# A Hawk and Conformer step: the order of every engine and the place of every tile taken from a list schedule in the source

## The chip, the cores and the metric

The kernel runs on one core of a Trainium2 chip. The core has five engines with their own instruction streams: TensorE (PE) for matrix products, VectorE (DVE), ScalarE (ACT), GpSimd (POOL), and SyncE (SP), which here only starts transfers. They meet at semaphores. The metric is the device time of one execution in microseconds; lower is better.

## The reference

1056 tokens (1024 of a prompt, then 8 samples of 4) go through two layers, each x + Mixer(RMSNorm(x)), and a last RMSNorm. D is 1024, the inner width 2048.

```python
# layer 0, Hawk
u = rmsnorm(x, g) @ w_in                      # [.., 4096]
xb, z = u[..., :2048], u[..., 2048:]
xb = causal_dwconv(xb, w of 4 taps) + b
r = sigmoid(einsum('bthi,hij->bthj', xb, w_a) + b_a)      # 16 blocks of 128 x 128
i = sigmoid(einsum('bthi,hij->bthj', xb, w_i) + b_i)
log_a = -8 * r * softplus(-lam);  a = exp(log_a)
b = sqrt(-expm1(2 * log_a)) * (i * xb)
h_t = a_t * h_(t-1) + b_t                     # scan over tokens
x = x + (h * silu(z)) @ w_out
# layer 1, Conformer
v, gl, z = split(rmsnorm(x, g) @ w_in + b_in)
c = v * sigmoid(gl)
c = silu(layernorm(causal_dwconv(c, w of 31 taps) + b))
x = x + (c * silu(z)) @ w_out + b_out
y = rmsnorm(x)
```

The states of both convolutions and of the scan are outputs too.

## The kernel before

Channels lie on the 128 partitions, tokens along the row. The 1056 tokens form three chunks of C = 352, one PSUM bank each. Inner channels form 16 blocks of 128, numbered s in layer 0 and j in layer 1. Weights come in slabs of 128 x 1024.

Products are made in a rounded 32-bit format with both sides split into a high part (a copy on ScalarE) and a low part (a subtraction on VectorE or GpSimd). So each term is three products, `high*high`, `high*low`, `low*high` (`mm`, three lines of matmuls). `w_conv` makes a slab's parts wh and wl. For 38 slabs of layer 1 the low part is made during layer 0 (`pre_low`: preh on ScalarE, pre on VectorE or GpSimd, then a store).

Layer 0, for each block s:

- X: three units of 24 products give xp, one for each chunk (`xb_unit`); ScalarE copies them to pad (`xb_evac`). `conv0` does the four taps (first on ScalarE into acc, then VectorE, the last into xc), `xc_split` the parts xcsh and xcsl.
- Z: three units give zp, `z_evac` puts SiLU of each chunk into zs.
- G: six gate units gp (`gate_unit`), three products and one sigmoid each, give r and i. `chain` goes on in steps q: 0 exponential a and tanh; 1 products on VectorE; 2 square root; 3 q times i; 4 the scan; 5 times zs; 6 the split into gsh and gsl. For block 15 steps 5 and 6 go by chunk.
- O: for a pair of blocks, half of its out products at a time: `out_unit`, six products into one bank op, and `out_evac`, in which VectorE adds the bank to x1.

The order by blocks is X4, Z4, O of an earlier pair, G4, and so on; the last steps are FINAL. The last two pairs' products go by chunk, together with the second norm (st: sums of squares by products; pb: the result spread over partitions). Layer 1 makes v, gl and z; cpad holds v times the sigmoid, spad the samples. VectorE does most of the 31 taps into cv, ScalarE and GpSimd 9 of them (prod, part). LayerNorm, the last products yp and the final norm follow.

Banks, tiles and order: 4 PSUM banks (mm) rotate among xp, zp, op and layer 1's products, 4 others (aux) among gates and sums. Rows of tokens live in 42 slots and 2 quick ones, small things in 10. A tile pool hands out places in rotation; who gets a used one waits for its last reader. Everything is put down as an event, and the sorted events are run:

```python
def at(t, fn, *a):
    ev.append((t, len(ev), fn, a))
for engines, a, b in ((SU_E, -1e9, SU_M), ((), SU_M, t_ordered), (MAN, t_ordered, 1e9)):
```

Before t = SU_M = 46 (startup) and from t_ordered on (the last chunks), the order of the events is each engine's order. Between them the framework's own scheduler reorders instructions by its estimate of when each could start. The three lines show the three stretches.

## Time and profile before

| | |
|---|---|
| Median of 3 runs | 1466.67 us (1466.05 to 1466.89) |
| Span of the profiled execution, first to last instruction | 1462.3 us |
| The runs' median less that span | 4.4 us |
| TensorE busy | 1398.0 us, 96% |
| VectorE busy | 1161.8 us, 79% |
| ScalarE, GpSimd busy | 872.4 and 872.5 us, 60% each |
| Mean granted TensorE clock | 0.986 |
| HBM read and written | 128.77 and 46.22 MB |

The profile is of one execution; the span leaves out what lies before the first and behind the last instruction. Busy time is the time in instructions, waiting is not counted. The granted clock is the share of full speed at which TensorE was let run. A line number is that of the kernel's source. A row of the timeline has start, duration, engine, line, operation, output and inputs; in brackets the idle time before it and what ended it. A row of a stretch gives for every engine its busy time with the number of instructions, then the clock, the DMA share and GB/s.

### The profile page before, as it was taken

What the parts mean: (1) busy time and instruction counts of PE and PEld (TensorE: products, weight loads), DVE (VectorE), ACT (ScalarE), POOL (GpSimd) and SP (SyncE); (2) the same over time, 40 slices, a digit from 0 to 9 for tenths busy, and PEclk for the clock granted to TensorE, in tenths of its full rate; (3) what the DMA queues carried; (4) which work ended last, traced back from release to release, by engine and by line L of the source; (5) the groups of instructions that cost most, each with busy time, mean ns of one, the idle gap of its engine ahead of it and who ended that gap; (6) DMA issues with size and microseconds to landing.
All of it is one profiled execution on the core that took longest, in us unless ns stands there. A gap on an engine that the chain in (4) does not pass through costs nothing.

```text
span 1462.3 us, 21525 instructions
## 1 busy us (share of the span) xinstructions
PE 1398.0 (96%) x8525; PEld 1367.2 (93%) x8525; DVE 1161.8 (79%) x1274; ACT 872.4 (60%) x1132; POOL 872.5 (60%) x479
## 2 busy tenths in 40 slices
...
GB/s 262 26 40 52 62 148 134 134 162 119 141 147 129 124 156 110 87 24 182 157 72 92 106 77 205 103 133 110 112 117 141 92 88 131 243 172 189 76 0 119
...
## 3 DMA queue, kind: packets, MB, share of 16 engines
...
q14 instruction: 34, 0.28, 0.1%
HBM read 128.77 MB, written 46.22 MB: 120 GB/s over the span
## 4 chain that ended last, share of the span: by engine, by line
DVE 25%; PE 22%; POOL 5%; issue 3%; ACT 3%; DMA 2%; SPq 0%; POOLq 0%; DVEq 0%; ACTq 0%
DVE cv__9086 L870 2%; DVE cv__10890 L870 2%; DVE cv__9391 L870 2%; DVE cv__8787 L870 2%; POOL part__7852 L832 1%; DMA co<-od 1%; DVE cv__10602 L870 1%; POOL part__8145 L832 1%; DVE co L1089 1%; DVE cv__7518 L870 1%; DVE cpad L816 1%; DVE cv__9687 L870 1%; DVE cv__11218 L870 1%; DVE cv__8491 L870 1%; DVE co L1085 1%
## 5 line engine op out<-in xcount | busy, mean ns | idle before, releaser
L827 ACT ACTIVATE prod<-cpad,lay 128x1024 f32<-128x1024 f32 x119 | 135.7, 1147 | 64.1 <-POOL part__8145 L832 7.7
L530 DVE SCALAR_TENSOR_TENSOR acc<-pad,par,acc 128x1080 f32<-128x1080 f32 x32 | 62.5, 1961 | 39.6 <-ACT acc L523 39.2
L612 POOL COPY st_h<-r 128x1 f32<-128x1 f32 x16 | 17.4, 1090 | 103.6 <-DVE r L611 103.6
L336 POOL TENSOR_TENSOR pre<-pre,preh 128x1024 f32<-128x1024 f32 x19 | 49.5, 2607 | 48.2 <-ACT preh L335 37.4
L542 POOL TENSOR_TENSOR gsl<-zs,gsh 128x1056 fp32r<-128x1056 f32 x15 | 37.1, 2474 | 26.3 <-ACT gsh L541 23.3
L1152 POOL TENSOR_TENSOR sq<-sq 128x512 f32<-128x512 f32 (+2 forms) x20 | 19.0, 953 | 56.4 <-ACT sq L1148 56.2
L1148 ACT ACTIVATE sq<-x 128x512 f32<-128x512 f32 (+2 forms) x23 | 11.4, 501 | 67.5 <-DVE x L1138 63.6
L336 DVE TENSOR_TENSOR pre<-pre,preh 128x1024 f32<-128x1024 f32 x19 | 30.3, 1593 | 26.2 <-ACT preh L335 26.2
L541 ACT ACTIVATE gsh<-zs 128x1056 fp32r<-128x1056 f32 x15 | 16.3, 1084 | 56.2 <-DVE zs L618 56.2
L541 ACT ACTIVATE xcsh<-xc 128x1056 fp32r<-128x1056 f32 x16 | 17.4, 1086 | 53.6 <-DVE xc L535 53.6
L894 POOL TENSOR_TENSOR sum<-sum,co 128x1056 f32<-128x1056 f32 x13 | 35.0, 2689 | 23.9 <-DVE co L870 15.4
L1093 ACT ACTIVATE co<-co,par 128x352 f32<-128x352 f32 (+1 forms) x24 | 22.7, 970 | 41.8 <-DVE co L1089 41.8
L335 ACT ACTIVATE preh<-pre 128x1024 fp32r<-128x1024 f32 x38 | 40.0, 1052 | 12.8 <-DMA pre<-win 12.6
L400 POOL TENSOR_TENSOR hl<-hn,hh 128x352 fp32r<-128x352 f32 x24 | 25.4, 1062 | 36.5 <-ACT hh L397 31.0
L879 POOL TENSOR_TENSOR smp<-spad,lay 128x992 f32<-128x992 f32 x16 | 40.1, 2504 | 4.3 <-DVE spad L815 4.3
L944 POOL TENSOR_TENSOR ssq<-ssq,sq 128x1056 f32<-128x1056 f32 x14 | 40.6, 2897 | 0.0
L594 DVE TENSOR_TENSOR i<-i,xc 128x1056 f32<-128x1056 f32 x16 | 31.4, 1965 | 10.2 <-ACT i L582 9.1
L604 DVE TENSOR_TENSOR q<-q,i 128x1056 f32<-128x1056 f32 x16 | 21.7, 1356 | 21.9 <-ACT q L601 21.9
L611 DVE TENSOR_TENSOR_SCAN r<-a,q 128x1056 f32<-128x1056 f32 x16 | 37.7, 2357 | 0.6
L1105 POOL TENSOR_TENSOR nl<-co,nh 128x1056 fp32r<-128x1056 f32 x6 | 16.6, 2767 | 34.3 <-ACT nh L1101 31.8
L1085 DVE TENSOR_TENSOR co<-co,mub 128x1056 f32<-128x1056 f32 (+1 forms) x20 | 25.3, 1289 | 10.8 <-DMA co<-od 7.9
L393 DVE SCALAR_TENSOR_TENSOR hn<-x,par,pb 128x352 f32<-128x352 f32 x48 | 25.5, 573 | 9.6 <-PE pb L285 5.2
...
## 6 DMA issues: line engine op xcount, KB each, us to landing
...
```

What stands on the lines that cost most here:

```text
L335: act.activation(h, r, AF.Copy)
L336: (dve if early[i] % PRED == PRED - 1 else pool).tensor_sub(r, r, h.bitcast(F))
L530: dve.scalar_tensor_tensor(acc, pad[:, k:k + n], w, acc, op0=OP.mult, op1=OP.add)
L541: act.activation(h, src, AF.Copy)
L542: lo.tensor_sub(l, src, h.bitcast(F))
L611: dve.tensor_tensor_scan(h, B["a", s], B["q", s], 0.0, op0=OP.mult, op1=OP.add)
L827: act.activation(p, B["c", j][:, k:k + NP], AF.Identity, scale=dw(j, k), bias=P("dw_b", j) if k == 0 else 0.0)
L870: dve.scalar_tensor_tensor(o, x, dw(j, k), y, op0=OP.mult, op1=OP.add)
L879: pool.tensor_mul(t_.rearrange("p (b t w) -> p b t w", b=NB, t=NS), win, wb)
L894: pool.tensor_add(B["sum"], B["sum"], B["o", j])
L944: (dve if j in SQD else pool).tensor_add(B["ssq"], B["ssq"], q)
L1085: dve.tensor_sub(d, d, B["mu", 0][:, :C] if c == 0 else B["mub"][:, w])
```

## The change

All engine calls are now recorded (`Eng`, `Plan.record`) instead of issued: each becomes an `Op` with an estimated duration, the operations it must follow (from the ranges of tiles that it reads and writes), and the tiles it needs. Consecutive matmuls of one event are one Op. `Plan.schedule` then builds the order of all five engines. The event time is an Op's due time, pulled ahead where a successor needs it earlier. At each step every engine looks at its next few Ops by due time (3 for PE, 30, 30, 20, 12), takes the first, or a later one that fits in before it; the earliest over all engines is placed. It accounts for table loads (1.3 us), for VectorE operations with two SBUF inputs and GpSimd's excluding each other, and for a DMA rate. A place (44 slots, 10 small ones, 4 + 4 banks) is given when an Op first needs it, the one that is free longest, and each has a tag of its own. `emit` issues everything in that order, for all five engines, from first to last.

```diff
+    def record(self, eng, name, fn, args, kw):
+        merge = eng == "PE" and self.last and self.last[0].eng == "PE" and self.last[1] == self.event
...
+        for o in ops:
+            o.due = o.at + SHIFT.get(o.key, 0.0)
+        for o in reversed(ops):
+            for s in o.succ:
+                o.due = min(o.due, s.due - o.dur - MARGIN - (T_DMA0 + T_DMAX + o.dma / DMA_BW if o.dma else 0))
...
+                    x = T_TABLE if o.func and o.func != table else 0.0
+                    s = max((max(free[e], last_end[e]) + x) if x else free[e], o.ready, c)
+                    if o.lock:
+                        s = max(s, lock)
+                    opts.append((s, x, o))
...
+                pick = opts[0]
+                for q in opts[1:]:
+                    back = T_TABLE if q[1] and pick[2].func and pick[2].func == table else 0.0
+                    if q[0] + q[2].dur + back + q[1] * 0.5 <= pick[0] + FIT[e]:
+                        pick = q
+                        break
+                s, x, o = pick
+                if best is None or s < best[0]:
+                    best = (s, x, o)
...
+    def emit(self, make, warm):
+        for o in self.seq:
+            for t in o.new:
+                t.real = make(t)
+            if o.warm:
+                warm(o.kind)
+            for fn, args, kw in o.parts:
+                fn(*[real(a) for a in args], **{k: real(a) for k, a in kw.items()})
...
+WIN = {"PE": 3, "DVE": 30, "Activation": 30, "Pool": 20, "SP": 12}
+LOOK = {"DVE": 20.0, "Activation": 20.0, "Pool": 20.0, "SP": 20.0}
+FIT = {"PE": 0.1, "DVE": 0.2, "Activation": 0.2, "Pool": 0.4, "SP": 0.1}
...
+        def warm(func):
+            nc.scalar.activation(spare.get()[:, 1:2], spare.get()[:, 0:1], func)
...
         def z_evac(s, c):
-            act.activation(B["zs", s][:, cs(c)], ps[:, :C], AF.Silu)
+            act.activation(B["zs", s][:, cs(c)], ps[:, :C], AF.Copy)
         def z_silu(s):
-            act.activation(B["zs", s][:, :C], B["zs", s][:, :C], AF.Silu)
+            act.activation(B["zs", s], B["zs", s], AF.Silu)
-        def gate_unit(s, u):
-            g, c = divmod(u, NCH)
...
-            ps = aux(f"gp{s}_{u}_")[:, :C]
-            mm(ps, [(h[:, g * 128:g * 128 + 128], l[:, g * 128:g * 128 + 128], xh[:, cs(c)], xl[:, cs(c)])])
...
+        def gate_units(s, g):
...
+            ps = [aux(f"gp{s}_{g}_{c}_")[:, :C] for c in range(NCH)]
+            for c in range(NCH):
+                mm(ps[c], [(h[:, g * 128:g * 128 + 128], l[:, g * 128:g * 128 + 128], xh[:, cs(c)], xl[:, cs(c)])])
+            for c in range(NCH):
+                act.activation(B["ri"[g], s][:, cs(c)], ps[c], AF.Sigmoid, bias=P("b_a" if g == 0 else "b_i", s))
...
             elif q == 2:
                 act.activation(B["q", s], B["q", s], AF.Sqrt)
+                if s not in late_z:
+                    z_silu(s)
...
-        flush(t_man)
+        flush()
```

`warm` puts a one-column activation on a constant tile `spare` ahead of each operation of another table, so that the table's load stands with it. SiLU of z is taken on the whole row of 1056 behind the square root of its block (behind its last z chunk in blocks 14 and 15). TensorE's 8472 matmuls are the same in number. Table loads are 91 instead of 101, with 90 one-column activations; 16 SiLUs of a whole row are added. On SP eight loads of x stand ahead of the first slab; before, it stood ahead of them; of neighbouring taps on VectorE, 101 pairs are on one accumulator instead of 64. Now every line of an engine's instruction is that of `emit` (L378) or `warm` (L455).

TensorE around the first gate of block 9, before (op3_4_1, for instance, is pair 3, out block 4, chunk 1; gp9_0 the first gate unit; the names behind are high and low parts):

```order
L244 MATMUL op3_4_2__3647<-gsh7_3139,wh27__3514 128x352
L245 MATMUL op3_4_2__3647<-gsl7_3140,wh27__3514 128x352
L246 MATMUL op3_4_2__3647<-gsh7_3139,wl27__3516 128x352
L244 MATMUL gp9_0__3731<-xcsh9_3582,gwh_3588 128x352
L245 MATMUL gp9_0__3731<-xcsl9_3583,gwh_3588 128x352
L246 MATMUL gp9_0__3731<-xcsh9_3582,gwl_3589 128x352
L244 MATMUL gp9_1__3739<-xcsh9_3582,gwh_3588 128x352
L245 MATMUL gp9_1__3739<-xcsl9_3583,gwh_3588 128x352
L244 MATMUL op3_5_0__3655<-gsh6_2769,wh27__3514 128x352
L245 MATMUL op3_5_0__3655<-gsl6_2770,wh27__3514 128x352
L246 MATMUL op3_5_0__3655<-gsh6_2769,wl27__3516 128x352
```

and after:

```order
L378 MATMUL op3_6_1_.0_3735<-gsh7.0_3290,wh27_.0_3453 128x352
L378 MATMUL op3_6_1_.0_3735<-gsl7.0_3294,wh27_.0_3453 128x352
L378 MATMUL op3_6_1_.0_3735<-gsh7.0_3290,wl27_.0_3486 128x352
L378 MATMUL gp9_0_0_.0_3743<-xcsh9.0_3670,gwh.9_3483 128x352
L378 MATMUL gp9_0_0_.0_3743<-xcsl9.0_3690,gwh.9_3483 128x352
L378 MATMUL gp9_0_0_.0_3743<-xcsh9.0_3670,gwl.9_3520 128x352
L378 MATMUL gp9_0_1_.0_3744<-xcsh9.0_3670,gwh.9_3483 128x352
L378 MATMUL gp9_0_1_.0_3744<-xcsl9.0_3690,gwh.9_3483 128x352
L378 MATMUL gp9_0_1_.0_3744<-xcsh9.0_3670,gwl.9_3520 128x352
L378 MATMUL gp9_0_2_.0_3745<-xcsh9.0_3670,gwh.9_3483 128x352
L378 MATMUL gp9_0_2_.0_3745<-xcsl9.0_3690,gwh.9_3483 128x352
L378 MATMUL gp9_0_2_.0_3745<-xcsh9.0_3670,gwl.9_3520 128x352
```

Before, three out products (op3_4_0 to op3_4_2) of that half stand between the last z product and the gate; after, eight (op3_4_0 to op3_6_1), and the gate's three chunks stand together, where op3_5_0 stood amid the second.

ScalarE at the end of layer 0, before (zp15_2 is the last z product, q15 the square root's row):

```order
L591 ACTIVATE a15_5791<-r15_5727,c8_79 128x1056
L592 ACTIVATE r15_5727<-r15_5727,c8_79 128x1056
L569 ACT_TABLE_LOAD
L569 ACTIVATE zs15_5798<-zp15_0__5760 128x352
L227 ACTIVATE wh46__5825<-wraw46__5765 128x1024
L569 ACTIVATE zs15_5798<-zp15_1__5800 128x352
L601 ACT_TABLE_LOAD
L601 ACTIVATE q15_5795<-q15_5795 128x1056
L569 ACT_TABLE_LOAD
L569 ACTIVATE zs15_5798<-zp15_2__5835 128x352
L227 ACTIVATE wh47__5865<-wraw47__5863 128x1024
L623 ACTIVATE gsh15_5870<-zs15_5798 128x352 x3
```

and after:

```order
L455 ACTIVATE spare_80<-spare_80 128x1
L378 ACTIVATE a15.0_5929<-r15.0_5838,c8_73 128x1056
L378 ACTIVATE r15.0_5838<-r15.0_5838,c8_73 128x1056
L378 ACTIVATE zs15.0_5857<-zp15_2_.0_5898 128x352
L378 ACTIVATE wh48_.0_5941<-wraw48_.0_5887 128x1024
L455 ACT_TABLE_LOAD
L455 ACTIVATE spare_80<-spare_80 128x1
L378 ACTIVATE q15.0_5944<-q15.0_5944 128x1056
L455 ACT_TABLE_LOAD
L455 ACTIVATE spare_80<-spare_80 128x1
L378 ACTIVATE zs15.0_5857<-zs15.0_5857 128x1056
L378 ACTIVATE gsh15.0_5962<-zs15.0_5857 128x352 x3
```

The square root stood ahead of the last z chunk's evacuation and a weight conversion, and stands behind both now; the whole row's SiLU and its table load stand between it and gsh15.

VectorE when the out products of pair 4 begin, before (x1_0 is out block 0; xcsl10 is the low part of block 10's convolution, pre a low part of layer 1's weights):

```order
L542 TENSOR_TENSOR xcsl10_3951<-xc10_3947,xcsh10_3950 128x1056
L646 TENSOR_TENSOR x1_0_88<-op4_0_0__3995,x1_0_88 128x352
L646 TENSOR_TENSOR x1_0_88<-op4_0_1__4003,x1_0_88 128x352
L646 TENSOR_TENSOR x1_0_88<-op4_0_2__4015,x1_0_88 128x352
L336 TENSOR_TENSOR pre_4046<-pre_4046,preh_4108 128x1024
L646 TENSOR_TENSOR x1_1_89<-op4_1_0__4023,x1_1_89 128x352
L646 TENSOR_TENSOR x1_1_89<-op4_1_1__4031,x1_1_89 128x352
L646 TENSOR_TENSOR x1_1_89<-op4_1_2__4039,x1_1_89 128x352
L646 TENSOR_TENSOR x1_2_90<-op4_2_0__4049,x1_2_90 128x352
L646 TENSOR_TENSOR x1_2_90<-op4_2_1__4057,x1_2_90 128x352
```

and after:

```order
L378 TENSOR_TENSOR x1_0.0_87<-op4_0_0_.0_4039,x1_0.0_87 128x352
L378 TENSOR_TENSOR x1_0.0_87<-op4_0_1_.0_4053,x1_0.0_87 128x352
L378 TENSOR_TENSOR x1_0.0_87<-op4_0_2_.0_4065,x1_0.0_87 128x352
L378 TENSOR_TENSOR xcsl10.0_4083<-xc10.0_4036,xcsh10.0_4063 128x1056
L378 TENSOR_TENSOR x1_1.0_89<-op4_1_0_.0_4075,x1_1.0_89 128x352
L378 TENSOR_TENSOR x1_1.0_89<-op4_1_1_.0_4087,x1_1.0_89 128x352
L378 TENSOR_TENSOR x1_1.0_89<-op4_1_2_.0_4095,x1_1.0_89 128x352
L378 TENSOR_TENSOR x1_2.0_92<-op4_2_0_.0_4103,x1_2.0_92 128x352
L378 TENSOR_TENSOR x1_2.0_92<-op4_2_1_.0_4111,x1_2.0_92 128x352
L378 TENSOR_TENSOR pre.23_4005<-pre.23_4005,preh.23_4073 128x1024
L378 TENSOR_TENSOR x1_2.0_92<-op4_2_2_.0_4133,x1_2.0_92 128x352
```

The first three additions to x1 stood behind xcsl10 and stand ahead of it now; a subtraction of pre stands between additions in both.

More of the change, by code (lines that the diff above doesn't have):

```diff
@@ L91, with __init__, _with, __getitem__ @@
 RMS_EPS, LN_EPS = 1e-6, 1e-5
+class V:
+    def __init__(self, tile_, ops, idx):
+        self.tile, self.ops, self.idx = tile_, ops, idx
+    def _with(self, op, idx):
+        return V(self.tile, self.ops + (op,), idx)
+    def __getitem__(self, key):
+        return self._with(lambda a: a[key], self.idx[key])
+    def bitcast(self, dt):
+        return self._with(lambda a: a.bitcast(dt), self.idx)
+    def to_broadcast(self, shape):
+        return self._with(lambda a: a.to_broadcast(shape), self.idx)
+    def rearrange(self, pat, **kw):
+        left = pat.split("->")[0]
+        shape = self.idx.shape
+        if "(" in left:
+            names = left[left.index("(") + 1:left.index(")")].split()
+            known = np.prod([kw.get(n, 1) for n in names])
+            shape = shape[:-1] + tuple(kw.get(n, int(shape[-1] // known)) for n in names)
+        else:
+            shape = (1, -1)
+        return self._with(lambda a: a.rearrange(pat, **kw), self.idx.reshape(shape))
+    def strided(self, shift, dims, step=lambda a: a.ap[0]):
+        n = int(np.prod([c for _, c in dims]))
+        span = 1 + sum(s * (c - 1) for s, c in dims)
+        flat = self.idx.reshape(-1)
+        idx = np.resize(flat[shift:shift + span], (1, max(n, span)))[:, :max(n, span)]
+        return self._with(lambda a: bass.AP(tensor=a.tensor, offset=a.offset + shift,
+                                            ap=[a.ap[0]] + [list(d) for d in dims]), idx)
+    def get(self):
+        a = self.tile.real
+        for op in self.ops:
+            a = op(a)
+        return a
+    @property
+    def n(self):
+        return self.idx.size
+    def span(self):
+        i = self.idx
+        return int(i.min()), int(i.max()) + 1
@@ new lines, with __init__, v @@
+class T:
+    def __init__(self, kind, name, shape, dt=F, real=None, phase=0, dram=False):
+        self.kind, self.name, self.dt, self.real, self.phase, self.dram = kind, name, dt, real, phase, dram
+        self.shape, self.left, self.free, self.place = shape, 0, 0.0, None
+        fake = [1 if q == 128 and i == (1 if dram else 0) else q for i, q in enumerate(shape)]
+        self.idx = np.arange(int(np.prod(fake))).reshape(fake)
+        self.users, self.hist = [], []
+    @property
+    def v(self):
+        return V(self, (), self.idx)
@@ new lines, with __init__ @@
+class Op:
+    __slots__ = ("eng", "parts", "due", "t", "pre", "succ", "left", "dur", "lock", "acc", "new", "dma", "start",
+                 "end", "func", "warm", "key", "kind", "n", "at", "ready", "tail")
+    def __init__(self, eng, at):
+        self.eng, self.at, self.parts, self.acc, self.pre, self.succ = eng, at, [], [], set(), []
+        self.dur, self.lock, self.dma, self.new, self.func, self.ready, self.warm = 0.0, False, 0, [], None, 0.0, False
+TABLE = {AF.Sigmoid: 1, AF.Exp: 2, AF.Tanh: 2, AF.Sqrt: 3, AF.Silu: 4}
@@ L115, in build @@
     nc = tc.nc
-    pe, act, dve, pool, sp = nc.tensor, nc.scalar, nc.vector, nc.gpsimd, nc.sync
+    plan = Plan(tc)
+    pe, act, dve, pool, sp = (Eng(plan, n, e) for n, e in zip(
+        ("PE", "Activation", "DVE", "Pool", "SP"), (nc.tensor, nc.scalar, nc.vector, nc.gpsimd, nc.sync)))
     from contextlib import ExitStack
@@ L191, in build, with flush @@
-        od = dr.tile([KI, 128, NT], F, name="od")
-        nss = cp.tile([128, NB * NS], F, name="nss")
-        wld = dr.tile([NPRE, 128, D], F, name="wld")
+        def flush():
+            for i, (t_, _, fn, args) in enumerate(sorted(ev, key=lambda e: e[:2])):
+                plan.at, plan.event = t_, i
+                plan.key = fn.__name__ + (str(args[1]) if fn in (chain, conv0) else "")
+                fn(*args)
+            plan.schedule({"s": NSLOT, "g": NSMALL, "mm": 4, "aux": 4, "c": 1})
+            with tc.manual_schedule(engines={getattr(mybir.EngineType, e) for e in ENG}):
+                plan.emit(make, warm)
@@ L732, in build @@
         at(t, softplus)
-        for s in range(2):
-            at(SU_Z + 0.1 * s, z_silu, s)
         wi = 4
```

293 lines of the change are left out of this document (237 added, 56 removed).

## The prediction

> **What bounds it now.** I read the page's shares first, then the busy time of each engine by stage, then TensorE's list of waits.
>
> ```profile
> PE 1398.0 (96%) x8525; PEld 1367.2 (93%) x8525; DVE 1161.8 (79%) x1274; ACT 872.4 (60%) x1132; POOL 872.5 (60%) x479
> ...
> core 0: us, PE busy (x) PEld busy (x) DVE busy (x) ACT busy (x) POOL busy (x), PEclk, DMA share, GB/s
> 0.00:61.00 61.00, 48.58 (x267) 46.57 (x268) 40.66 (x72) 34.04 (x69) 22.18 (x30) 0.94 0.45 160
> 61.00:629.00 568.00, 544.23 (x3326) 536.41 (x3324) 391.45 (x428) 368.66 (x471) 261.36 (x187) 0.99 0.32 114
> 629.00:634.00 5.00, 1.60 (x7) 1.49 (x8) 4.89 (x7) 2.15 (x4) 3.31 (x3) 0.89 0.32 117
> 634.00:692.00 58.00, 55.80 (x339) 55.20 (x338) 44.36 (x84) 36.73 (x70) 32.03 (x26) 0.95 0.31 114
> 692.00:1221.00 529.00, 524.08 (x3211) 512.75 (x3210) 519.41 (x447) 350.62 (x410) 462.07 (x186) 1.00 0.36 112
> 1221.00:1240.00 19.00, 16.59 (x101) 15.50 (x100) 13.81 (x28) 9.77 (x13) 10.52 (x5) 0.91 0.55 165
> 1240.00:1452.00 212.00, 205.38 (x1274) 198.07 (x1272) 141.38 (x197) 70.22 (x97) 80.44 (x46) 1.00 0.38 135
> 1452.00:1462.30 10.30, 1.71 (x12) 1.23 (x10) 5.81 (x19) 0.20 (x1) 0.55 (x1) 0.67 0.51 175
> ```
>
> TensorE is the bound: 1398.0 of 1462.3 us. The change leaves every product in place, so all it can win on TensorE is the 64.3 us of idle time and what runs at the lower clock. The stages share the idle time so: startup (to 61) 12.4, layer 0 (61 to 629) 568.00 - 544.23 = 23.8, the end of layer 0 3.4, layer 1's entry 2.2, the convolution 4.9, LayerNorm 2.4, output products 6.6, tail 8.6. In layer 0 every other engine has much room (VectorE 391 of 568). In the convolution VectorE is busy 519 of 529 us: there TensorE and VectorE are both nearly full, and time that VectorE gains or loses shows.
>
> ```profile
> engine line waited for: us in total, times, longest us
> PE xp__184 L244 <- ACT hh L412: 6.2, 1, 6.2
> PE op__1459 L244 <- DVE x L646: 3.5, 1, 3.5
> PE op__5881 L244 <- ACT gsh L623: 3.4, 1, 3.4
> PE gp__2997 L244 <- ACT xcsh L541: 3.4, 1, 3.4
> PE st L258 <- DVE acc L294: 2.9, 1, 2.9
> PE op__3671 L244 <- DVE x L646: 2.0, 1, 2.0
> ...
> PE op__5603 L244 <- DVE x L646: 1.9, 1, 1.9
> PE gp__1296 L244 <- ACT r L582: 1.8, 1, 1.8
> ...
> PE op__1861 L244 <- DVE x L646: 1.7, 1, 1.7
> ```
>
> Layer 0's waits are of two kinds: a gate product (gp) that waits for the split convolution xcsh or for a bank that a sigmoid still reads, and an out product (op) that waits until VectorE has added an earlier one to x, which frees its PSUM bank. Some of them also cost clock, as these stretches of 10 us show (the column behind the busy times is the granted clock):
>
> ```profile
> 143.00:153.00 10.00, 6.54 (x31) 6.25 (x31) 9.96 (x13) 1.08 (x1) 2.69 (x3) 0.83 0.18 53
> 298.00:308.00 10.00, 6.57 (x27) 6.28 (x26) 6.36 (x6) 4.00 (x6) 2.92 (x2) 0.69 0.55 207
> 388.00:398.00 10.00, 8.00 (x50) 7.70 (x49) 7.07 (x9) 5.61 (x9) 3.23 (x3) 1.00 0.59 213
> 586.00:596.00 10.00, 7.66 (x36) 7.09 (x36) 10.00 (x13) 9.62 (x10) 2.05 (x1) 0.83 0.28 102
> 629.00:639.00 10.00, 6.60 (x31) 6.49 (x32) 8.47 (x14) 5.14 (x10) 7.25 (x6) 0.83 0.16 59
> ```
>
> A clock of 0.83 over 10 us costs 1.7 us, 0.69 costs 3.1. In layer 0 that is 1.7 + 3.1 + 1.7 = 6.5 us, at 143, 298 and 586. With the idle time, 23.8 + 6.5 = 30.3 us are to be had there.
>
> **Layer 0's gates and out products.** In the new order of TensorE (shown for block 9) a block's first gate stands five out products of six matmuls further behind its x products: 120 matmuls between them instead of 90, so in blocks 5 to 13 (block 7 had 76). One takes 544.23 / 3326 = 0.164 us, so xcsh and xcsl have 19.6 us instead of 14.7. How long they take, for block 11:
>
> ```profile
> 453.08 0.42 ACT L515 ACTIVATE pad<-xp__4208 128x320 f32<-128x320 f32 x1
> ...
> 462.37 1.26 DVE L542 TENSOR_TENSOR xcsl<-xc,xcsh 128x1056 fp32r<-128x1056 f32 x1 [1.15 <-ACT xcsh L541]
> ```
>
> 463.63 - 453.08 = 10.6 us, well inside both. The worst gate, block 7's, waited 3.4 us (gp__2997) behind its 76 matmuls (12.5 us): its split came 15.9 us after the products and would fit too, by 3.7 us. The gates' waits go. The waits for sigmoids go as well: three products, then three sigmoids, and the SiLU table is no longer loaded in between, since the z banks are now left by a copy.
>
> The out products' waits go less surely. Three out products (18 matmuls, 2.9 us) stand between two uses of a bank in both orders, and VectorE's rows (pair 4) show that an addition to x no longer stands behind xcsl of the next block but still has a subtraction `pre` in front of it here and there. The subtraction waits for GpSimd and for ScalarE's conversion. I leave two waits of the size of the smaller ones above (1.9 + 1.7) and one stretch at 0.83 (1.7): 5.3 us. Gain 30.3 - 5.3 = 25.0; ends: 30.3 if nothing waits, 18.2 if the additions' four waits (3.5 + 2.0 + 1.9 + 1.7 = 9.1) and 3.0 of clock stay.
>
> The Trainium skill (TensorE: Matmul & The Clock Gate, "What's actually happening") has the clock halved after at least one idle window of some 3.4 us in free-running windows. By that rule short leftover waits cost no clock, and the 5.3 would be 3.6. The trace differs: the 1.9 us wait of op__5603 is followed by 0.83, the 2.0 us wait of op__3671 by 1.00. So I keep the 1.7.
>
> **ScalarE's added work.** 90 activations of one column, each under the 0.46 us of a 128x352 copy (below), are under 41 us; 16 SiLUs of a whole row at the 1.09 of the square root below are 17; ten table loads fewer at 1.28 are -13. That is at most 45 us over the kernel, mostly in layer 0, where ScalarE is idle for 568 - 369 = 199 us: nothing, as long as no chain waits for it. Loading tables ahead is worth nothing either, since loads ran beside other waits already. One chain does wait.
>
> **The end of layer 0.** The last pair's out products wait for gsh of block 15:
>
> ```profile
> 623.03 1.28 ACT L601 ACT_TABLE_LOAD   x1
> 624.33 1.09 ACT L601 ACTIVATE q<-q 128x1056 f32<-128x1056 f32 x1
> ...
> 626.73 0.46 ACT L569 ACTIVATE zs<-zp__5835 128x352 f32<-128x352 f32 x1
> 627.09 1.05 ACT L227 ACTIVATE wh__5865<-wraw__5863 128x1024 fp32r<-128x1024 f32 x1
> 631.85 1.37 ACT L623 ACTIVATE gsh<-zs 128x352 fp32r<-128x352 f32 x3 [3.72 <-DVE zs L622]
> ...
> 626.95 2.36 DVE L611 TENSOR_TENSOR_SCAN r<-a,q 128x1056 f32<-128x1056 f32 x1
> 629.41 3.28 DVE L622 TENSOR_TENSOR zs<-zs,r 128x352 f32<-128x352 f32 x3
> ```
>
> Before, the square root ended at 625.42, ahead of the last z product, and gsh began 6.4 us later. In the new order it stands behind that product's copy and a weight conversion: copy to 627.19, conversion to 628.2, load 1.28, a column (under 0.46), root 1.09, which makes 630.8: 5.4 us later. The SiLU behind it (load 1.28 + 1.09, to 633.2) lies beside the scan, which would end at 629.41 + 5.4 = 634.8. Next late is the product z*r: its three parts took 3.28 us, although gsh shows that the first came only at 631.85; undisturbed, a part has 0.46 as on ScalarE, and 2.0 us come back. So TensorE waits 3.4 to 5.4 us more, and perhaps one more stretch at half clock (1.7): +3.4 to +7.1, I take +5.
>
> The Trainium skill (ScalarE: Activation LUTs, "What ACT_TABLE_LOAD costs") puts a switch at 1283 ns plus a drain of about 1380 ns; by it the term would be +6.4. The trace has 1.28 us and the next activation 0.02 us behind it (623.03, 624.33), so I take the trace.
>
> **Startup.** The first product waits 6.2 us now, st waits 2.9 later, and 0.94 over 61 us is 3.7 us of clock. In the new order eight loads of x stand on SP's queue ahead of the first weight slab, so TensorE begins later; then less is waited for. At the 160 GB/s of this stage eight loads of 176 KB are 8.8 us; half of it is +4.4, and -2.9 for st with half of the clock, -1.8, make about 0. Ends -3 and +3.
>
> **Layer 1's entry and convolution.** st and pb of the second norm now stand back to back with no product between: up to the 2.9 of st above and 1.7 of clock, I take +2.
>
> ```profile
> 700.60 10.56 DVE L870 SCALAR_TENSOR_TENSOR cv__6610<-cpad,lay,cv__6610 128x1024 f32<-128x1024 f32 x8
> ...
> 1007.81 1.28 DVE L870 SCALAR_TENSOR_TENSOR cv__9391<-cpad,lay,cv__9391 128x1024 f32<-128x1024 f32 x1
> 1009.00 1.28 DVE L870 SCALAR_TENSOR_TENSOR cv__9086<-cpad,lay,cv__9086 128x1024 f32<-128x1024 f32 x1
> ...
> L815 DVE TENSOR_TENSOR spad<-v,g 128x32 f32<-128x32 f32 x16 | 14.7, 920 | 6.1 <-ACT v L802 6.1
> L816 DVE TENSOR_TENSOR cpad<-v,g 128x1024 f32<-128x1024 f32 x16 | 27.5, 1719 | 0.0
> L879 POOL TENSOR_TENSOR smp<-spad,lay 128x992 f32<-128x992 f32 x16 | 40.1, 2504 | 4.3 <-DVE spad L815 4.3
> ```
>
> Taps that follow on their own accumulator cost 10.56 / 8 = 1.32 us, on another 1009.00 - 1007.81 = 1.19. In the new order 101 stand so instead of 64: 37 x 0.13 = +4.9 on VectorE, with no cover. Against it: spad, with a 32nd of cpad's work, takes 0.92 us, and cpad 1.72 where a tap of its size takes 1.28. VectorE waits there while GpSimd reads, some 16 x (0.44 + 0.87) = 21 us. The list schedule lets neither start while the other holds; I credit half, -10.4. Sum 2 + 4.9 - 10.4 = -3.5. It cannot win more than what TensorE has there, 2.2 + 4.9 idle and 58 x 0.05 = 2.9 of clock, -10; without the credit it is +9.5 at most.
>
> **Rest.** LayerNorm and output products have 2.4 + 6.6 idle and 19 x 0.09 = 1.7 of clock; no row says which the order gives back: -4, of 0 to -10.7. The tail waits for the last stores: 0.
>
> **Sum.** -25.0 + 5 + 0 - 3.5 - 4 = -27.5 on a span of 1462.3: 1434.8. The runs' median 1466.67 lies 4.4 above that span; with it, 1439.2, so 1439. Its own range, 1428 to 1452, takes layer 0's ends, the entry's and the startup's.
>
> **Rivals.** Deeper: the list schedule also empties what I left. Layer 0's 5.3, startup 3, the convolution's other 6.5 and 2 of the rest make -17: 1422. For it: all of this is idle time with free engines beside it. Against: VectorE is 98% busy in the convolution.
>
> Nothing gained: only the gates' waits go, since bank releases depend on contention that no order fixes. Of 23.8, the four additions' 9.1 and another 3.0 of waits for ScalarE stay, the clock too: -11.7; the end gives +5, the taps +4.9: 1465. Against: the additions no longer stand behind xcsl.
>
> Slower: the new order puts VectorE's operations with two inputs in SBUF more often against GpSimd's. In the convolution 63 of them (cpad, spad, partial sums, copies to co) stand in the order; by the rows above each waits 0.4 to 0.9 us now, and GpSimd is busy 462 of 529 us in operations of 2.5 us. Had one always to wait for the half, it would be 1.25 us, for all of it 2.5. At 0.5 to 0.7 more each, 63 x = +32 to +44 on VectorE, which has no slack: 1471 to 1483. It decides from (1469.6 - 1439) / 63 = 0.49 us more for each. For it: the change reorders just these engines. Against: the taps' order from blocks is nearly the same. The Trainium skill (SBUF — State Buffer, "SBUF: two separate sides") calls the port these two share an exclusive lock for the whole instruction; spad's 0.92 us agrees.
>
> **Chances.** Forecast 0.55, deeper 0.20, nothing 0.08, slower 0.17. A difference under 0.2% (1463.7 to 1469.6) is about what a measurement of this kernel cannot tell from none. Faster 0.75, same 0.08, slower 0.17. The range from 1420 to 1468 leaves out the slower case.
>
> **What would show it.** Right: the stage 61 to 629 is some 25 us shorter, with no gate among the longest waits; the wait of the last pair for gsh of block 15 is 7 to 9 us; tap pairs on one tile are more, cpad's and spad's means lower. Wrong: long waits of out products for x; a stage of the convolution over 540 us with cpad near 2.2; a first product after 15 us that is not won back by 61.

## The result, and the profile after

The changed kernel takes 1475.54 us (median of 14 runs, 1468.59 to 1481.14); the kernel before, run beside it, 1466.78 (14 runs, 1464.05 to 1471.11). The ratio is 1.0055, with a 95% interval from 1.0042 to 1.0069: slower by half a per cent, where the forecast was 1439. The profiled execution has a span of 1473.7 us.

The page's first part, then busy times in stretches cut where the changed kernel's stages end (columns as before):

```profile
PE 1392.1 (94%) x8525; PEld 1370.0 (93%) x8525; DVE 1175.3 (80%) x1274; ACT 887.4 (60%) x1226; POOL 868.0 (59%) x480
...
61.00:620.00 559.00, 535.39 (x3303) 532.07 (x3301) 405.60 (x404) 376.75 (x527) 259.35 (x181) 0.98 0.34 116
620.00:632.00 12.00, 0.32 (x1) 0.29 (x1) 10.55 (x11) 7.48 (x12) 4.24 (x4) 0.68 0.19 67
632.00:706.00 74.00, 65.27 (x379) 63.72 (x379) 48.02 (x93) 37.14 (x74) 32.18 (x26) 0.91 0.27 97
706.00:1247.00 541.00, 527.18 (x3208) 515.87 (x3207) 508.89 (x441) 350.23 (x427) 460.92 (x188) 0.98 0.40 114
1247.00:1466.00 219.00, 217.45 (x1377) 212.70 (x1375) 152.24 (x229) 78.08 (x111) 82.02 (x48) 1.00 0.39 138
```

TensorE is still the bound, and from 1247 on it hardly waits at all. Over the span it is idle 81.6 us instead of 64.3 (+17.3). It works 37.6 us at half the clock instead of 32.4, and half of such time is lost (+2.6). Its products follow each other a little more closely, which makes the other -8.5 of the 11.4 us between the two spans. What it waits for, longest first:

```profile
PE zp_.0_211 L378 <- ACT wh_.0_176 L378: 12.2, 1, 12.2
PE op_.0_5972 L378 <- ACT gsh15.0_5962 L378: 11.8, 1, 11.8
PE op_.0_1495 L378 <- DVE x_0.0_87 L378: 8.7, 1, 8.7
PE op_.0_5710 L378 <- DVE x_2.0_92 L378: 7.7, 1, 7.7
PE gp_.0_10509 L378 <- ACT z2.0_10505 L378: 4.6, 1, 4.6
PE gp_.0_9935 L378 <- ACT z1.0_9930 L378: 4.6, 1, 4.6
PE st.5_6518 L378 <- DVE acc.7_6303 L378: 4.5, 1, 4.5
PE vp_.0_8066 L378 <- ACT g6.0_8058 L378: 3.8, 1, 3.8
PE op_.0_3352 L378 <- DVE x_0.0_87 L378: 2.8, 1, 2.8
```

Before, apart from the first product, nothing was above 3.5 us. Six of these nine (op 1495, 5710 and 3352 for x, the two gp and vp for z and g) are for a PSUM bank that another engine still has to read. The gates of layer 0 are not in the list: that part came as forecast.

The end of the same product in both executions tells where time was won and lost:

| product | before | after | ahead (-) or behind |
|---|---|---|---|
| x products of block 3 | 106.31 | 106.92 | +0.6 |
| pair 5, first chunk of out block 6 | 547.51 | 532.07 | -15.4 |
| x products of block 15 | 576.37 | 566.48 | -9.9 |
| pair 6, last chunk of out block 3 | 596.81 | 591.58 | -5.2 |
| last pair, last chunk of out block 3 | 664.69 | 671.16 | +6.5 |
| v of block 0, layer 1 | 693.35 | 706.05 | +12.7 |
| z of block 9, layer 1 | 1221.74 | 1247.05 | +25.3 |
| third group, out block 1 | 1369.36 | 1380.82 | +11.5 |
| last of all | 1455.62 | 1467.02 | +11.4 |

The order differs too: at the second point 12 products fewer have run than before (some 2 us), at the others at most 5. So layer 0 won 14 to 16 us and kept none of it, layer 1's entry lost 6, the convolution 12.6, and the LayerNorm and output products gave back 13.9.

What a bank wait looks like, on VectorE ahead of the out product that came at 150.25 (first column start, second duration, brackets the idle time before):

```profile
137.73 0.53 DVE L378 TENSOR_TENSOR x_0.0_87<-op_.0_1429,x_0.0_87 128x352 f32<-128x352 f32 x1 [0.46 <-PE op_.0_1429 L378]
138.17 1.89 DVE L378 SCALAR_TENSOR_TENSOR acc4.0_1424<-pad4.0_1357,par,acc4.0_1424 128x1080 f32<-128x1080 f32 x1
...
146.03 2.36 DVE L378 TENSOR_TENSOR_SCAN r2.0_1348<-a2.0_1453,q2.0_1474 128x1056 f32<-128x1056 f32 x1
148.48 1.28 DVE L378 TENSOR_TENSOR zs2.0_953<-zs2.0_953,r2.0_1348 128x1056 f32<-128x1056 f32 x1
149.68 0.51 DVE L378 TENSOR_TENSOR x_0.0_87<-op_.0_1437,x_0.0_87 128x352 f32<-128x352 f32 x1
...
150.25 0.66 PE L378 MATMUL op_.0_1495<-gsh0.0_1125,wh_.0_1313 128*128 128x352 f32 x1 [8.70 <-DVE x_0.0_87 L378]
```

Between the second addition to x (137.73) and the third (149.68) stands the rest of block 2's chain, scan included, with two taps of block 4. All four banks are full, and TensorE waits for an addition of half a microsecond. In the convolution it is ScalarE. Before, z of layer 1's block 2 left its first bank 2.3 us after its products' end (1083.93), chunk by chunk:

```profile
1086.26 0.55 ACT L804 ACTIVATE z<-zp__10217,par 128x352 f32<-128x352 f32 x1
1089.74 0.55 ACT L804 ACTIVATE z<-zp__10265,par 128x352 f32<-128x352 f32 x1
1093.65 0.53 ACT L804 ACTIVATE z<-zp__10302,par 128x352 f32<-128x352 f32 x1
```

Now the three leave together behind a run of tap products and weight conversions, one table load for all, the first of them 16.2 us after its products' end (1102.09):

```profile
1113.85 1.13 ACT L378 ACTIVATE prod_8.0_10493<-cpad13.0_10217,lay.1_5956 128x1024 f32<-128x1024 f32 x1
1114.89 1.04 ACT L378 ACTIVATE wh_.0_10497<-wraw_.0_10397 128x1024 fp32r<-128x1024 f32 x1
1115.83 1.04 ACT L378 ACTIVATE wl_.0_10500<-wlow_.0_10399 128x1024 fp32r<-128x1024 f32 x1
1116.88 1.28 ACT L455 ACT_TABLE_LOAD   x1
1118.28 0.54 ACT L378 ACTIVATE z2.0_10505<-zp_.1_10336,par 128x352 f32<-128x352 f32 x1
...
1118.87 0.66 PE L378 MATMUL gp_.0_10509<-hh.8_6165,wh_.0_10144 128*128 128x352 f32 x1 [4.64 <-ACT z2.0_10505 L378]
```

Most of these waits stand in the order itself: the list schedule has an estimate of its own for every start, and its table holds gaps on TensorE at these places and of about this size.

| wait | in the schedule's table | on the chip |
|---|---|---|
| pair 0, out block 2 (op_.0_1495) | 9.0 | 8.7 |
| pair 6 (op_.0_5710) | 7.9 | 7.7 |
| gsh of block 15 | 13.9 | 11.8 |
| bank of z1, of z2 | 4.7, 4.9 | 4.6, 4.6 |

Not all of them do: for st.5 and for pb.5 behind it the table has 1.3 and 3.6 where the chip waited 4.5 and 1.8, for g6 nothing where it waited 3.8. And the table ends at 1438.7, while the chip's span is 1473.7; half the clock, which the schedule does not know, is 18.8 of these 35 us.

### The profile page after: what moved, and what is told of

It is laid out like the page before. It is cut to its first block, busy times and chain, and to the rows that moved or that the text cites. A ratio compares the mean times of both kernels' runs of the same rounds, so it can differ in the third digit from the quotient of the medians.

```text
span 1473.7 us, 21670 instructions
## 1 busy us (share of the span) xinstructions
PE 1392.1 (94%) x8525; PEld 1370.0 (93%) x8525; DVE 1175.3 (80%) x1274; ACT 887.4 (60%) x1226; POOL 868.0 (59%) x480
## 4 chain that ended last, share of the span: by engine, by line
PE 36%; DVE 9%; ACT 4%; issue 1%; POOL 1%; ACTq 0%; POOLq 0%; DVEq 0%
DVE cv_.0_7047 L378 2%; DVE cv_.0_6732 L378 2%; DVE cv_.0_7418 L378 1%; DVE cv_.0_7710 L378 1%; DVE cv_.0_9530 L378 1%; POOL part_.0_6944 L378 0%; PE gp_.0_9935 L378 0%; DVE cv_.0_9261 L378 0%; PE gp_.0_10509 L378 0%; PE vp_.0_8066 L378 0%; ACT L455 0%; PE zp_.1_11177 L378 0%; PE vp_.0_10229 L378 0%; PE vp_.0_9314 L378 0%; PE gp_.0_8698 L378 0%
## 5 line engine op out<-in xcount | busy, mean ns | idle before, releaser
L378 DVE SCALAR_TENSOR_TENSOR cv_.0_6732<-cpad0.0_6525,lay.1_5956,cv_.0_6732 128x1024 f32<-128x1024 f32 x25 | 32.2, 1287 | 0.5
L378 DVE SCALAR_TENSOR_TENSOR cv_.0_7047<-cpad1.0_6615,lay.1_5956,cv_.0_7047 128x1024 f32<-128x1024 f32 x23 | 29.5, 1283 | 0.2
L378 DVE SCALAR_TENSOR_TENSOR cv_.0_10685<-cpad13.0_10217,lay.1_5956,cv_.0_10685 128x1024 f32<-128x1024 f32 x20 | 25.8, 1288 | 1.8 <-PE cv_.0_10685 L378 1.3
L378 DVE SCALAR_TENSOR_TENSOR cv_.0_10081<-cpad11.0_9641,lay.1_5956,cv_.0_10081 128x1024 f32<-128x1024 f32 x20 | 25.7, 1283 | 1.4 <-PE cv_.0_10081 L378 1.1
L378 DVE SCALAR_TENSOR_TENSOR cv_.0_9835<-cpad10.0_9312,lay.1_5956,cv_.0_9835 128x1024 f32<-128x1024 f32 x20 | 25.7, 1286 | 1.2 <-PE cv_.0_9835 L378 0.8
L378 DVE SCALAR_TENSOR_TENSOR cv_.0_8951<-cpad7.0_8486,lay.1_5956,cv_.0_8951 128x1024 f32<-128x1024 f32 x20 | 25.6, 1280 | 1.2 <-PE cv_.0_8951 L378 1.1
L378 DVE SCALAR_TENSOR_TENSOR cv_.0_10410<-cpad12.0_9963,lay.1_5956,cv_.0_10410 128x1024 f32<-128x1024 f32 x20 | 25.7, 1285 | 0.7 <-PE cv_.0_10410 L378 0.5
L378 DVE SCALAR_TENSOR_TENSOR cv_.0_9261<-cpad8.0_8765,lay.1_5956,cv_.0_9261 128x1024 f32<-128x1024 f32 x20 | 25.7, 1283 | 0.7 <-PE cv_.0_9261 L378 0.6
L378 DVE SCALAR_TENSOR_TENSOR cv_.0_10987<-cpad14.0_10534,lay.1_5956,cv_.0_10987 128x1024 f32<-128x1024 f32 x20 | 25.8, 1288 | 0.5
L378 DVE SCALAR_TENSOR_TENSOR cv_.0_9530<-cpad9.0_8984,lay.1_5956,cv_.0_9530 128x1024 f32<-128x1024 f32 x20 | 25.7, 1283 | 0.6 <-PE cv_.0_9530 L378 0.4
L378 DVE SCALAR_TENSOR_TENSOR cv_.0_7418<-cpad2.0_6898,lay.1_5956,cv_.0_7418 128x1024 f32<-128x1024 f32 x20 | 25.6, 1282 | 0.1
L378 DVE SCALAR_TENSOR_TENSOR cv_.0_8641<-cpad6.0_8053,lay.1_5956,cv_.0_8641 128x1024 f32<-128x1024 f32 x20 | 25.6, 1280 | 0.1
L378 DVE SCALAR_TENSOR_TENSOR cv_.0_7710<-cpad3.0_7149,lay.1_5956,cv_.0_7710 128x1024 f32<-128x1024 f32 x20 | 25.5, 1277 | 0.1
L378 DVE SCALAR_TENSOR_TENSOR cv_.0_8281<-cpad5.0_7715,lay.1_5956,cv_.0_8281 128x1024 f32<-128x1024 f32 x19 | 24.3, 1277 | 0.2 <-DVE cv_.0_8641 L378 0.2
L378 DVE SCALAR_TENSOR_TENSOR cv_.0_8015<-cpad4.0_7449,lay.1_5956,cv_.0_8015 128x1024 f32<-128x1024 f32 x19 | 24.3, 1278 | 0.0
L455 ACT ACTIVATE spare<-spare 128x1 f32<-128x1 f32 x90 | 18.3, 203 | 1.0
L378 DVE SCALAR_TENSOR_TENSOR cv_.0_11284<-cpad15.0_10845,lay.1_5956,cv_.0_11284 128x1024 f32<-128x1024 f32 x12 | 15.5, 1289 | 0.4
L378 DVE TENSOR_TENSOR zs14.0_5772<-zs14.0_5772,r14.0_5592 128x1056 f32<-128x1056 f32 x1 | 1.3, 1261 | 17.8 <-ACT zs14.0_5772 L378 17.8
L378 POOL TENSOR_TENSOR gsl14.0_5891<-zs14.0_5772,gsh14.0_5889 128x1056 fp32r<-128x1056 f32 x1 | 2.5, 2462 | 18.4 <-ACT gsh14.0_5889 L378 18.4
L378 POOL TENSOR_TENSOR sq.54_13297<-sq.54_13297,sq.55_13313 128x512 f32<-128x512 f32 x1 | 1.3, 1291 | 19.0 <-ACT sq.55_13313 L378 19.0
L378 ACT ACTIVATE sq.54_13297<-x_0.0_11713 128x512 f32<-128x512 f32 x1 | 0.6, 632 | 19.6 <-DVE x_0.0_11713 L378 19.6
```

The costliest lines, as they stand in the source:

```text
L378: fn(*[real(a) for a in args], **{k: real(a) for k, a in kw.items()})
L455: nc.scalar.activation(spare.get()[:, 1:2], spare.get()[:, 0:1], func)
```

## The experiments

Theory A is that the losses are waits that the schedule's ranking makes: each engine takes the operation with the earliest due date first, and an evacuation that TensorE needs now has a later date than a chain or a run of conversions that is itself overdue. Its rival B is that the chip runs later than any such plan (VectorE and GpSimd keeping each other out), so that a fixed order waits somewhere. All comparisons are with runs of the kernel before on the same chip, whose median lay between 1466.8 and 1470.6.

**Layer 1's evacuations earlier.**

```diff
-SHIFT = {}
+SHIFT = {"l1_evac": -6.0}
```

> Layer 1's evacuations (and, through them, their products) get a due time 6 earlier in the list schedule; nothing else is touched. Theory A, the waits stand in the order itself (an evacuation ranks by its event time and is put behind a run of conversions and tap products; the next product needs its bank, but the schedule's due times follow data alone, not banks): the three waits in the convolution (3.8, 4.6, 4.6 us) go, with up to 8.5 us of half clock behind them, so 12 to 21 us less than the changed kernel, 1455 to 1464. Theory B, the engines run later than the schedule estimates (VectorE and GpSimd keeping each other out) and any fixed order waits somewhere: under 4 us, the waits turn up at other products.

1447.3 us, ratio 0.9855 (0.9825 to 0.9885) to the kernel before. The waits for g6, z1 and z2 are gone (3.8 + 4.6 + 4.6), and so is that of st.5 (4.5), which had not been counted. Behind the four TensorE had worked 3.2, 5.4, 3.8 and 5.1 us at half the clock, which cost half of that, 8.7. Together they make 26 us; the gain was 28, more than theory A's 12 to 21. Layer 0 keeps its waits:

```profile
PE op_.0_5974 L378 <- ACT gsh15.0_5962 L378: 11.8, 1, 11.8
PE op_.0_1495 L378 <- DVE x_0.0_87 L378: 8.7, 1, 8.7
PE op_.0_5710 L378 <- DVE x_2.0_92 L378: 7.7, 1, 7.7
PE op_.0_3352 L378 <- DVE x_0.0_87 L378: 2.7, 1, 2.7
```

**Additions to x higher in rank.**

```diff
-SHIFT = {}
+SHIFT = {}
+BOOST = {"out_evac": 4.0}
...
+        for o in ops:
+            o.due -= BOOST.get(o.key, 0.0)
         queues = {e: sorted((o for o in ops if o.eng == e), key=lambda o: o.due) for e in ENG}
```

> VectorE's additions of the out products (out_evac) rank 4 earlier in the list schedule, their products stay where they were. Theory A: the waits of 8.7 us at 141 and 7.7 us at 582 shrink to under 5 together, with 3 to 6 us of half clock; the wait for gsh of block 15 stays, as its gates hang on the same products. 8 to 18 us less than the changed kernel, 1457 to 1467. Theory B: under 4 us.

1451.96 us, ratio 0.9886 (0.9850 to 0.9923): 24 us less than the changed kernel, more than the 8 to 18 of theory A. In place of the 8.7 a later product of the pair waits 4.3, the 7.7 went, the two smaller ones for x went too, and the wait for block 15 stayed:

```profile
PE op_.0_5974 L380 <- ACT gsh15.0_5962 L380: 10.4, 1, 10.4
...
PE op_.0_1542 L380 <- DVE x_2.0_92 L380: 4.3, 1, 4.3
```

**Block 15's gates earlier.**

```diff
-SHIFT = {}
+SHIFT = {"last_gates": -20.0}
...
                 plan.key = fn.__name__ + (str(args[1]) if fn in (chain, conv0) else "")
+                if fn is gate_units and args[0] == KI - 1:
+                    plan.key = "last_gates"
```

> Only the due time of block 15's gate products is 20 earlier. Theory A: block 15's chain is what the last out products wait for; it begins with these gates, which the schedule put 162 products behind the x products instead of 78, so the wait of 11.8 us for gsh shrinks to 7 to 9 and the half clock behind it too: 5 to 12 us less than the changed kernel, 1463 to 1470. Theory B (the chain's length is what VectorE and GpSimd make of it, it stays as long behind the last z product): under 3 us.

1460.84 us, ratio 0.9949 (0.9930 to 0.9969), 15 us less, more than theory A's 5 to 12. The wait for gsh is 5.1 us, with 2.3 for gsl behind it, and the 7.7 us of op_.0_5710 went too, which was not expected: the schedule is made anew from the place of the change on.

```profile
PE op_.0_5972 L378 <- ACT gsh15.0_5960 L378: 5.1, 1, 5.1
```

**The three together.** The edits of the three above, with -10.0 for the gates.

> The three together (layer 1's evacuations 6 earlier, the additions 4 higher in rank, block 15's gates 10 earlier). Theory A: the gains add up but for what the chain of block 15 takes back: 22 to 38 us less than the changed kernel, 1437 to 1453, faster than the kernel before. Theory B: under 10 us, still slower than the kernel before.

1426.97 us, ratio 0.9718 (0.9690 to 0.9746): 49 us less than the changed kernel and 41 less than before. That is below theory A's range. TensorE is busy 97%. B is out as the main cause: a fixed order on the same engines, with the same estimates, waits little.

```profile
PE 1380.6 (97%) x8525; PEld 1360.7 (96%) x8525; DVE 1155.8 (81%) x1274; ACT 887.6 (62%) x1226; POOL 867.7 (61%) x480
...
PE op_.0_5972 L380 <- ACT gsh15.0_5962 L380: 7.6, 1, 7.6
PE op_.0_1542 L380 <- DVE x_2.0_92 L380: 4.3, 1, 4.3
PE op_.0_1820 L380 <- POOL gsl3.0_1812 L380: 1.9, 1, 1.9
```

**Rank alone in layer 1.** As for the additions, with another name:

```diff
+BOOST = {"l1_evac": 6.0}
```

> In layer 1 only the rank of the evacuations is 6 higher in the changed kernel's schedule; their products stay where they were. Theory A in its plain form (rank alone frees the banks): the three waits of 3.8 to 4.6 us go as when evacuations and products moved together, 1445 to 1456. Theory L (ScalarE switches tables for each evacuation then, and taps, conversions and LayerNorm's sums come later; the schedule's own table has waits of up to 6 us at the sums of the convolution): slower than the changed kernel, 1478 to 1492.

1486.91 us, ratio 1.0114 (1.0072 to 1.0155), 11 us slower than the changed kernel, as theory L had it. (ScalarE loads 91 tables in both, so more frequent switches are not the reason.) In layer 1 it is not rank alone: the wait for z2 stays, one as long for z0 (4.7) comes in place of that for z1, and new ones stand at the convolution's sums and at pb of the second norm.

```profile
PE cv_.0_8645 L380 <- DVE cv_.0_8645 L380: 6.1, 1, 6.1
PE pb.5_6537 L380 <- DVE sm L380: 4.8, 1, 4.8
PE gp_.0_10509 L380 <- ACT z2.0_10505 L380: 4.7, 1, 4.7
```

The due dates in the changed kernel's schedule show why rank does not help z2. Its first evacuation is due at 929.0 and is the first in ScalarE's queue from 1073.0 of the table on. But it needs a table load, 1.3 us in the schedule, and 13 tap products and conversions of 0.95 to 1.13 us that are due later (932.8 to 958.7) pass it one by one, since each would end before z2 could start. On the chip they are the rows from 1103.52 to 1115.83. z1 is passed in the same way. So theory A's account holds for the additions to x: that of 149.68 is due at 106.9, behind block 2's chain at 94.7 to 106.7. For z1 and z2 the cause is not a later due date, but the rule by which a later operation may pass. A schedule without that rule on ScalarE was not run.

**Parts of the change without the list schedule.** `gate_units` and the whole-row SiLU of the change, word for word, in the kernel before.

> The kernel before, with its own order, plus two parts of the change alone: a gate's three products together and then its three sigmoids, and SiLU of z on whole rows behind the square root. Theory A (the order of the list schedule makes the difference, of both signs): within 6 us of the kernel before, 1461 to 1473. Theory C (these parts carry layer 0's gain, since the gates no longer wait): 1450 to 1460, with no gate over 1.5 us among TensorE's waits. Theory D (they make the end of layer 0 longer): over 1473, with a wait for gsh of block 15 of 6 us or more.

1474.97 us, ratio 1.0048 (1.0028 to 1.0068). These parts carry no gain. The time is that of theory D, but its mechanism is only partly there: the wait for gsh of block 15 is 4.5 us where before it was 3.4, and a gate still waits 3.4. A new wait for VectorE's taps (4.6) and 4 us less of TensorE's work between 61 and 560 stand beside it; which of the two parts does it was not tried.

```profile
PE cv__9701 L937 <- DVE cv__9701 L875: 4.6, 1, 4.6
PE op__5895 L244 <- ACT gsh L625: 4.5, 1, 4.5
PE op__1871 L244 <- DVE x L648: 3.7, 1, 3.7
PE gp__3003 L244 <- ACT xcsh L541: 3.4, 1, 3.4
```

**SiLU of z by chunk in the list schedule.**

```diff
-            act.activation(B["zs", s][:, cs(c)], ps[:, :C], AF.Copy)
+            act.activation(B["zs", s][:, cs(c)], ps[:, :C], AF.Silu)
...
-            act.activation(B["zs", s], B["zs", s], AF.Silu)
+            if s < 2:
+                act.activation(B["zs", s][:, :C], B["zs", s][:, :C], AF.Silu)
```

> The list schedule as it is, but SiLU of z is taken chunk by chunk as z leaves its banks, as in the kernel before (no SiLU of whole rows). The schedule is made anew from it. Theory A: the wait for gsh of block 15 is 3 to 4 us shorter, since one table load and one whole-row SiLU leave that chain; the waits for banks in the convolution stay. 3 to 10 us less than the changed kernel, 1466 to 1473. Theory H (whole rows save table loads that layer 0 needs): 1479 or more.

1464.0 us, ratio 0.9982 (0.9966 to 0.9998): 11.5 us less than the changed kernel, a little more than theory A's 3 to 10. The wait for gsh went from 11.8 to 7.6, and those for x from 8.7 and 7.7 to 6.9 and 5.0; the bank waits of the convolution stayed (4.6, 4.6, 4.2). SiLU on whole rows cost the changed kernel time.

**No one-column activations.**

```diff
-            if o.warm:
-                warm(o.kind)
```

> The changed kernel without the 90 one-column activations that pull a table's load ahead; order and places are the same. Theory A (loads run ahead of their operation's wait anyway, and ScalarE has room): within 4 us of the changed kernel, 1471 to 1480. Theory G (a load then stands behind the wait for its operation's input): 1.3 us more wherever such an operation is on the chain that TensorE waits for, the waits for gsh of block 15 and for z1 and z2 in the convolution 1 to 3 us longer, 1480 or more.

1477.34 us, ratio 1.0065 (1.0043 to 1.0086), beside 1.0055 with them. Loading tables ahead did nothing to the time that can be told apart. Theory G's mechanism can be seen all the same: without them the waits of 8.7 and 7.7 us are 10.0 and 9.0, 1.3 us more each, and in block 2's chain the load stands behind the wait for its input (142.12, the square root at 143.42). The first product's wait is 1.3 us shorter (10.9), and that for gsh is 11.6.

**The kernel before without its hand order at the end.**

```diff
-        flush(t_man)
+        flush()
```

> The kernel before without its hand-written order from t_man on: the framework's scheduler also orders the LayerNorm, the output products and the final norm. The changed kernel made up 14 us there. Theory E (the hand order cost it): 1453 to 1463. Theory F (it takes the list schedule): 1464 or more, with TensorE's idle time from 1221 on at 15 us or more.

1470.91 us, ratio 1.0025 (1.0007 to 1.0043). It is no gain, so dropping the hand order does not explain what the changed kernel won from the LayerNorm on (13.9 us); what is left for it is the list schedule, with its order and its places. From 1221 to its end at 1466.9 TensorE was busy 226.7 us and idle 19, as F had it.

**The schedule without its rule on VectorE and GpSimd.**

```diff
-                    if o.lock:
-                        s = max(s, lock)
```

> The changed kernel's schedule without its rule that a VectorE operation with two inputs in SBUF and a GpSimd operation exclude each other; it is made anew without the rule. Theory M (the rule is what shortened VectorE's waits in the convolution: the sixteen cpad from 1.72 us to 1.34, the sixteen spad from 0.92 to 0.47): they go back to 1.6 or more and 0.8 or more, VectorE's time in the convolution grows by over 8 us. Theory N (they became shorter for another reason, by standing elsewhere): within 0.15 us of the changed kernel's. The whole time hangs on where the bank waits fall in this order too and is no test of either: 1460 to 1490.

1533.46 us, ratio 1.0436 (1.0400 to 1.0471), far outside the range that was given for the time. The rule that the two exclude each other is worth 58 us here, with new waits for banks of up to 7.5 us. From the first product of cpad to the last tap VectorE is busy 531.8 us instead of 499.7. The sixteen cpad took 1.58 us in the mean instead of 1.34, but spad 0.52 beside 0.47, so M holds for VectorE's time and for cpad in direction (it had 1.6 or more), and not for spad. The taps that add GpSimd's sum grew most, from 1.75 to 2.50 (15 each).

**All that gained.** The three together (evacuations 5.0, additions 5.0, gates 10.0) and SiLU by chunk.

> All that gained, together: layer 1's evacuations 5 earlier, the additions 5 higher in rank, block 15's gates 10 earlier, SiLU of z chunk by chunk. Theory A: the wait for gsh of block 15 (7.6 us with the first three) shrinks by 1 to 3 us and some half clock goes: 2 to 8 us less than those three together (1427), 1419 to 1425. Theory I (the gains overlap, since the chain of block 15 takes back what is won ahead of it): within 2 us of 1427.

1423.49 us, ratio 0.9679 (0.9644 to 0.9713); the wait for gsh is 6.5 us. That is in theory A's range, but the three together ran on another chip and the intervals of the two ratios overlap, so A is not told from I.

**And the first slab first.**

```diff
-FIT = {"PE": 0.1, "DVE": 0.2, "Activation": 0.2, "Pool": 0.4, "SP": 0.1}
+FIT = {"PE": 0.1, "DVE": 0.2, "Activation": 0.2, "Pool": 0.4, "SP": 0.0}
```

> As the kernel with all four, and the first weight slab is loaded ahead of x again: SP's rule that a later operation may jump ahead if it delays the first by no more than 0.1 is off for SP (issuing takes it 0.06, so the rule always lets the second in line pass, and the first slab, due first, came 31st). Theory J (startup is bound by all its loads, the first product's 12 us are won back by 61): within 2 us of the kernel with all four. Theory K (the late first product costs what it is later): 4 to 6 us faster.

1420.61 us, ratio 0.9661 (0.9628 to 0.9695), the fastest of all, 50 us below the kernel before on the same chip. The first product comes at 6.3 again, and 2.9 us remain of the 5.6: between J and K.

```profile
PE op_.0_5961 L380 <- ACT gsh15.0_5949 L380: 6.5, 1, 6.5
PE xp_.0_226 L380 <- ACT hh.0_147 L380: 6.3, 1, 6.3
PE op_.0_1541 L380 <- DVE x_2.0_95 L380: 1.8, 1, 1.8
```

## Why the prediction was wrong

**Startup, 0: right.** The first product waited 12.2 us instead of 6.2, and by the x products of block 3 the kernels were 0.6 us apart. Why the first slab came so late was not seen; the last experiment shows it: a rule by which the second in line may always pass.

**Layer 0, -25: the gates right, the out products wrong.** No gate of layer 0 waits above 0.8 us, and at 532 the kernel is 16.0 us ahead of where it was (15.4 and the startup's 0.6; some 2 of it are products that now come later). The step that failed is "I leave two waits of the size of the smaller ones above": four additions made TensorE wait 8.7, 2.8, 2.0 and 7.7 us instead of 1.9 and 1.7, and half the clock cost 5.3 there instead of 1.7. That step was read off pair 4, where the new order is good, and carried over to the others. In pair 0 and pair 6 an addition stands behind a whole chain of VectorE operations. The order shows that; the place that was shown was typical and not the worst.

**The end of layer 0, +5: wrong in its mechanism.** The term put the copy of the last z chunk and a weight conversion ahead of the square root. They stood there and cost nothing: both were done by 621.6, and the root waited 2.4 us for VectorE, whose q15 took 3.19 us (1.26 before, at 620.19) beside a subtraction of GpSimd (621.66 to 624.33):

```profile
622.26 3.19 DVE L378 SCALAR_TENSOR_TENSOR q15.0_5944<-q15.0_5944,r15.0_5838 128x1056 f32<-128x1056 f32 x1
...
625.48 1.08 ACT L378 ACTIVATE q15.0_5944<-q15.0_5944 128x1056 f32<-128x1056 f32 x1 [2.38 <-DVE q15.0_5944 L378]
```

The chain hangs on block 15's gates, and they ended at 610.53 before and 610.83 after. The last product ahead of the wait in TensorE's timeline and the one that needs gsh, of before and of after:

```profile
628.64 0.32 PE L246 MATMUL op__5933<-gsh,wl__5827 128*128 128x352 f32 x1
632.40 0.43 PE L244 MATMUL op__5881<-gsh,wh__5825 128*128 128x352 f32 x1 [3.45 <-ACT gsh L623]
```

```profile
619.59 0.32 PE L378 MATMUL op_.0_5972<-gsh14.0_5889,wl_.0_5923 128*128 128x352 f32 x1
631.68 0.66 PE L378 MATMUL op_.0_5972<-gsh15.0_5962,wh_.0_5860 128*128 128x352 f32 x1 [11.77 <-ACT gsh15.0_5962 L378]
```

gsh came at nearly the same time in both (631.85, 631.13). TensorE reached the place 9 us earlier and waited 8.3 us longer, so the gain that layer 0 still had was used up there. Counted from the end of the last z product, gsh came 12.7 us later instead of 9.8: 2.8 us more, where the term had 3.4 to 5.4. The other 5.5 us are the step that the term left out: what TensorE has to run in the meantime. Before, 36 products that do not need block 15 ran between the last z product and the wait, nine for each of four banks; now it is nine in all, 27 fewer, which at 0.16 us each are 4.3 of the 5.5. In the list the twelve products of a bank are one Op, so they stay together, and the next banks' products stand behind them. That was read off the rows, and no run tried it. Half the clock began inside the wait and lasted 13.7 us; the 6.2 us of it in which TensorE worked cost 3.1, where before 3.4 us cost 1.7. From -5.2 to +6.5 the place cost 11.7 us, more than twice the term. Block 15's gates stand 162 products behind its x products instead of 78; the prediction counted distances for blocks 5 to 13 alone.

**ScalarE's added work, 0: half right.** The one-column activations cost nothing. The whole-row SiLUs did cost: by chunk, in a schedule made anew, the kernel is 11 us faster, with 4.2 us less of waiting for gsh and 4.5 less at the two long waits for x.

**Entry and convolution, -3.5: wrong.** VectorE did win what the term credits: sixteen cpad 21.4 us instead of 27.5, sixteen spad 7.5 instead of 14.7, together 13.3 where 10.4 was credited, and dropping the rule costs VectorE 32 us. The step that failed is that the term counted VectorE's work alone. TensorE was as full (524 of 529 us), and the release of its four banks by ScalarE was not looked at; the first bank of z2 was held for 16.2 us after its products. The waits for g6, z1 and z2, 13.0 us, and the half clock behind them made the convolution +12.6. The entry's mechanism was right and its size wrong (+6.2, 2 was taken): with no product between, st.5 waited 4.5 us for the sums (acc.7) and pb.5 1.8.

**The rest, -4: mis-sized.** It gave 13.9, more than the 10.7 that was set as its bound. All the idle time and the half clock there went (up to the third group TensorE is idle 0.0 us instead of 9.0); the rest are products that follow each other more closely, which the bound did not hold.

**The rivals.** The slower one ended on the right side with the wrong mechanism: VectorE's waits for GpSimd in the convolution became shorter. That 1475.5 lies in its 1471 to 1483 is luck. Of "nothing gained" the core was right, that bank releases can take back what the gates win, but it expected them to stay as they were, not to grow.
